# Up-projection of a hybrid layer: high and low words of each weight interleaved in SBUF

## The chip, the cores and the metric

The kernel runs on one core of a Trainium2 chip. The metric is the device time of one execution in microseconds; the time before is 2269.59 us, the median of three runs (2268.82 to 2269.59).

## The reference

One layer of a streaming encoder for 2048 prompt tokens and 8 x 16 sample tokens: mLSTM heads and windowed attention over one input projection, an output projection, a layer norm, and then a convolutional feed-forward part. Only the start of that last part is touched by the change:

```python
def conv_ffn(h, conv_prev, w_up, w_conv, b_conv, w_down):
    T = h.shape[1]
    u = h @ w_up                      # (T, 1024) @ (1024, 2 * 2816)
    ext = jnp.concatenate([conv_prev.astype(u.dtype), u], axis=1)
    c = b_conv + sum(ext[:, j:j + T] * w_conv[j] for j in range(CONV_W))
    a, g = jnp.split(c, 2, axis=-1)
    return (jax.nn.silu(g) * a) @ w_down, ext[:, -(CONV_W - 1):]
```

All inputs and outputs are float32, and so is the product `h @ w_up`.

## The kernel before

The 2048 + 128 tokens are 17 tiles of 128. The kernel has four stages, one after the other: input projection (with mLSTM and attention woven in), output projection, up-projection (`f_ups`), down-projection (`f_downs`). Each float32 product is made of float32r matmuls: `split` (L220) writes a high part of an operand with ScalarE (a cast to float32r, L222) and the remainder with VectorE (a subtraction, L223), and three matmuls add high x high, high x low and low x high in PSUM.

The up-projection goes over three blocks of tokens (`FBLOCKS`: 6, 6 and 5 tiles), and in each block over 22 pairs j of 128 value columns and 128 gate columns of `w_up`. A pair is a 2 x 2 block product (two halves of the contraction, value and gate, two halves of the tokens) done with seven products instead of eight, numbered s = 1 to 7, on sums of the operands. A product (`f_product`, L1894) contracts over 512: four steps k of 128, and at each step three matmuls, with the weights stationary (128 x 128, high, high, low) and half of the block's tokens moving (384 columns, 320 in the last block). That is 12 matmuls a product, 7 x 22 x 3 = 462 products, 5544 matmuls, all at L1902. They go to six PSUM banks, three named `fup` and three named `dps`, used by odd and even pairs in turn.

`self.seq` holds the order of the products, written out by hand (`ORDER`), and the TensorE program follows it. `f_next` (L1806) prepares the weights of one product: it takes the next of ten slots of 1088 words per partition (`f_slot`, of which 1024 words from word 48 on are used) and fills it with the high part and the low part of a [128, 4, 128] quarter, 512 words each. It runs `AHEAD` = 6 products ahead of TensorE in the first block and 8 in the others. Where the weights come from differs:

- In the first block every quarter is split on the chip. Products 6, 5, 7 and 3 use sums of quarters, which VectorE makes first (L1819 to L1822), and what was split for them is also stored to DRAM (`zw`, L1837).
- In the later blocks those four are loaded from `zw` (L1830, 512 KB each), and only products 1, 2 and 4 are split again from the raw weights `wv` and `wg`.

Beside this VectorE makes the sums of the results (`f_evict`), the depthwise convolution (L1960) and the gate (L1986, L1987); ScalarE copies PSUM banks and makes the first term of the convolution (L1958) and the tanh. All loads and stores of the stage are issued by SyncE's queue (SP). `f_written` (L1889) issues two extra matmuls of 512 columns with a weight slot as stationary operand.

Of the kernel before, what the change touches and what calls it, by code (L numbers as in the profile page):

```python
# [8 lines left out]
F32 = mybir.dt.float32  # L9
# [197 lines left out]
class Prog:  # L207
# [1598 lines left out]
    def f_next(self):  # L1806

        nc, V = self.nc, self.nc.vector
        if self.made >= len(self.seq):
            return False  # L1810
        b, j, s = self.seq[self.made]
        self.made += 1
        if s == 1:
            if (b, j) not in self.wr:
                self.f_raw(b, j)
            if b == 0:
                v, g = self.wr[b, j]
                s12, s34 = self.f_slot(48, F32), self.f_slot(48, F32)
                V.tensor_add(s12[:, :4], g[:, :4], g[:, 4:])  # L1819
                V.tensor_sub(s34[:, :4], v[:, :4], g[:, :4])  # L1820
                V.tensor_sub(s12[:, 4:], s12[:, :4], v[:, :4])
                V.tensor_sub(s34[:, 4:], v[:, 4:], s12[:, 4:])  # L1822
                self.wr[b, j] = v, g, s12, s34
        if s == 5 and (b, j) != (len(FBLOCKS) - 1, NFF - 1):
            self.f_raw(b + (j + 1) // NFF, (j + 1) % NFF)
        w = self.f_slot(48).rearrange("p (i k) m -> p i k m", i=2)
        i = SUMS.index(s) if s in SUMS else None
        keep = None if i is None else self.zw[j][i].rearrange("p (i k m) -> p i k m", i=2, k=4)
        if b and i is not None:
            nc.sync.dma_start(w.bitcast(F32), keep)  # L1830
        else:
            r = self.wr[b, j]
            q = {1: lambda: r[0][:, :4], 2: lambda: r[0][:, 4:], 4: lambda: r[1][:, 4:], 5: lambda: r[2][:, :4],
                 6: lambda: r[2][:, 4:], 7: lambda: r[3][:, :4], 3: lambda: r[3][:, 4:]}[s]()
            self.split(w[:, 0], w[:, 1], q)
            if i is not None:
                nc.sync.dma_start(keep, w.bitcast(F32))  # L1837
        self.wc[b, j, s] = w[:, 0], w[:, 1]
        return True

# [395 lines left out]
```

## Time and profile before

| what | value |
|---|---|
| time, median of 3 runs | 2269.59 us |
| the profiled execution: time | 2270.08 us |
| the profiled execution: span from first to last instruction | 2268.3 us |
| granted TensorE clock over the span | 0.999 |
| up-projection matmuls (L1902), first start to last start | 886.8 to 1810.1 us |
| DMA traffic over the span | 631.30 MB, mean 278 GB/s |

The profile gives for each engine the time in which it was busy; PE is the matmuls and PEld the loads of the stationary operand, which run beside them. Both are pipelined: a matmul's own duration is longer than the distance between the starts of two matmuls, so the rate is read from starts or from pieces of the chain that hold many matmuls, not from durations. A group's line gives line, engine, operation, names, shape and count, then busy time, mean duration of one in ns, and the idle time of the engine before them. The chain of work is followed back from the last instruction; its pieces have a start, a length and a count.

### The profile page before, as it was taken

What the parts mean: (1) busy time and instruction counts of PE and PEld (TensorE: products, weight loads), DVE (VectorE), ACT (ScalarE), POOL (GpSimd) and SP (SyncE); (2) the same over time, 40 slices, a digit from 0 to 9 for tenths busy, and PEclk for the clock granted to TensorE, in tenths of its full rate; (3) what the DMA queues carried; (4) which work ended last, traced back from release to release, by engine and by line L of the source; (5) the groups of instructions that cost most, each with busy time, mean ns of one, the idle gap of its engine ahead of it and who ended that gap; (6) DMA issues with size and microseconds to landing.
All of it is one profiled execution on the core that took longest, in us unless ns stands there. A gap on an engine that the chain in (4) does not pass through costs nothing.

```text
span 2268.3 us, 39783 instructions
## 1 busy us (share of the span) xinstructions
PE 2251.2 (99%) x14293; PEld 2081.9 (92%) x14293; DVE 1807.6 (80%) x3069; ACT 1273.1 (56%) x2374; POOL 270.3 (12%) x509
## 2 busy tenths in 40 slices
PE   9999999999999999999999999999999999999998
PEld 8999999999878778999999999999999988888887
DVE  9787687777698888998778777678766787896997
ACT  5453476776776656555656555556555644444452
POOL 0001001000021110211112000003211200100100
PEclk9999999999999999999999999999999999999999
DMA  8888998898997767898777999988998796757752
GB/s 304 315 314 317 317 320 275 277 315 294 331 325 262 275 216 282 305 330 302 279 284 261 308 307 311 314 274 277 316 304 263 253 318 207 255 188 234 247 171 89
DMA packets 302277, 631.30 MB, mean 278 GB/s; under 512 B 47420, under 2 KB 140672, under 8 KB 302080
## 3 DMA queue, kind: packets, MB, share of 16 engines
q1 hardware_dynamic: 296832, 614.01, 78.9%
q0 software_dynamic: 3520, 10.56, 1.5%
q10 hardware_dynamic: 1728, 4.20, 0.5%
q8 instruction: 113, 1.85, 0.3%
q14 instruction: 84, 0.69, 0.1%
HBM read 457.02 MB, written 171.64 MB: 277 GB/s over the span
## 4 chain that ended last, share of the span: by engine, by line
PE 80%; DVE 5%; issue 1%; ACT 1%; DMA 1%; POOL 0%; DVEq 0%; SPq 0%; ACTq 0%; POOLq 0%
PE dps L1902 20%; PE fup L1902 20%; PE dps L726 8%; PE fup L2112 7%; PE dps L2112 7%; PE fht L2112 5%; PE dps L227 2%; PE dps L228 2%; PE dps L229 2%; PE ppo L1372 1%; PE dps L752 1%; PE psc L1327 1%; PE ppt L1366 1%; DVE w L223 1%; PE fht L1724 1%
## 5 line engine op out<-in xcount | busy, mean ns | idle before, releaser
L1902 PE MATMUL fup<-hh,uw 128*128 128x384 f32 (+1 forms) x1848 | 476.8, 327 | 0.0
L1902 PE MATMUL dps<-hh,uw 128*128 128x384 f32 (+1 forms) x1848 | 476.7, 327 | 0.0
L1902 PEld LDWEIGHTS fup<-hh,uw 128*128 128x128 f32 x1848 | 329.6, 188 | 0.1
L1902 PEld LDWEIGHTS dps<-hh,uw 128*128 128x128 f32 x1848 | 329.5, 188 | 0.0
L1902 PE MATMUL fup<-hl,uw 128*128 128x384 f32 (+1 forms) x924 | 301.9, 327 | 1.2 <-DVE hl L223 1.2
L1902 PE MATMUL dps<-hl,uw 128*128 128x384 f32 (+1 forms) x924 | 301.7, 327 | 0.0
L1960 DVE SCALAR_TENSOR_TENSOR cc<-u,cw,cc 128x768 f32<-128x768 f32 (+1 forms) x264 | 258.1, 978 | 38.5 <-ACT cc L1958 32.1
L726 PE MATMUL dps<-w,oh 128*128 128x256 f32 x1344 | 251.2, 283 | 0.2 <-ACT dps L820 0.2
L222 ACT CAST uw<-wraw 128x1024 fp32r<-128x1024 f32 x126 | 123.9, 983 | 216.1 <-PE dps L2112 117.9
L223 DVE TENSOR_TENSOR w<-wraw,w 128x1024 fp32r<-128x1024 f32 (+2 forms) x163 | 186.5, 1150 | 63.8 <-ACT w L222 61.7
L222 ACT CAST w<-wraw 128x1024 fp32r<-128x1024 f32 (+2 forms) x163 | 160.7, 992 | 110.8 <-PE dps L726 55.4
L726 PEld LDWEIGHTS dps<-w,oh 128*128 128x128 f32 x1344 | 209.7, 188 | 11.3 <-issue 8.1
L726 PE MATMUL dps<-w,ol 128*128 128x256 f32 x672 | 187.1, 278 | 0.0
L223 DVE TENSOR_TENSOR uw<-wraw,uw 128x1024 fp32r<-128x1024 f32 x126 | 142.3, 1129 | 53.8 <-ACT uw L222 53.7
L1902 PEld LDWEIGHTS fup<-hl,uw 128*128 128x128 f32 x924 | 173.6, 188 | 1.9 <-DVE hl L223 1.8
L1902 PEld LDWEIGHTS dps<-hl,uw 128*128 128x128 f32 x924 | 173.6, 188 | 0.0
L726 PE MATMUL dps<-oh,w 128*128 128x256 f32 x896 | 167.4, 283 | 2.0 <-ACT mr L1177 0.9
L2112 PE MATMUL fup<-uw,fu 128*128 128x512 f32 x726 | 168.9, 389 | 0.0
L2112 PEld LDWEIGHTS fup<-uw,fu 128*128 128x128 f32 x726 | 136.3, 188 | 28.3
L2112 PE MATMUL dps<-uw,fu 128*128 128x512 f32 x660 | 160.7, 389 | 0.0
L2112 PEld LDWEIGHTS dps<-uw,fu 128*128 128x128 f32 x660 | 123.9, 188 | 25.8
L726 PEld LDWEIGHTS dps<-oh,w 128*128 128x128 f32 x896 | 139.8, 188 | 7.9 <-issue 4.1
(319 smaller groups left out, 4555.8 us busy)
## 6 DMA issues: line engine op xcount, KB each, us to landing
uw<-zw SPq DMA_DIRECT2D x176, 512.0 KB, 5.1
zw<-uw SPq DMA_DIRECT2D x88, 512.0 KB, 3.4
w<-zws SPq DMA_DIRECT2D x72, 512.0 KB, 5.9
wv<-wup SPq DMA_DIRECT2D x66, 512.0 KB, 5.3
wraw<-wi SPq DMA_DIRECT2D x65, 512.0 KB, 5.3
wraw<-zt SPq DMA_DIRECT2D x60, 512.0 KB, 3.8
wraw<-wdn SPq DMA_DIRECT2D x45, 512.0 KB, 3.9
wraw<-wo SPq DMA_DIRECT2D x40, 512.0 KB, 4.4
```

The lines of the kernel that those rows point to most:

```text
L222: nc.scalar.copy(hi, src)
L223: return nc.vector.tensor_sub(lo, src, hi.bitcast(F32)).ins
L227: mm(out, ah, bh, start=start, stop=False)
L228: mm(out, ah, bl, start=False, stop=False)
L229: mm(out, al, bh, start=False, stop=stop)
L726: mm(o, l, r, start=s in (1, 7) and c == k == i == 0, stop=k == 3 and i == 2, skip_group_check=True)
L752: mm(o, x, w, start=k == i == 0, stop=k == KD - 1 and i == 2, skip_group_check=True)
L1327: nc.tensor.matmul(ps[kvh][:, j, :nk], q[rs, j0 + j], k[rs, sel], start=i == 0, stop=i == 2)
L1366: nc.tensor.transpose(pp[:, j * P:(j + 1) * P], scs[j // 2][:, 2 * kvh + j % 2, kt * P:(kt + 1) * P], self.ident)
L1902: mm(ps, l[:, k], r[:, k], start=s in (1, 7) and k == 0 and i == 0, stop=k == 3 and i == 2, skip_group_check=True)
L1960: V.scalar_tensor_tensor(c[:, v], u[:, i:i + n], w[i], c[:, v], op0=ALU.mult, op1=ALU.add)
L2112: mm(ps, l[:, k, c], r[:, k], start=s in (1, 4, 7) and u == 0 and k == 0 and i == 0, stop=u == nu - 1 and k == n - 1 and i == 2, skip_grou ...
```

## The change

Where a slot held 512 words of the high part and behind them 512 words of the low part, it now holds them word by word: high and low part of the same weight are neighbours. The two operands are views of one tile, with a step of two words:

```diff
-        w = self.f_slot(48).rearrange("p (i k) m -> p i k m", i=2)
+        both = self.f_slot(48).rearrange("p k m -> p (k m)")
+        w = both.rearrange("p (k m i) -> p i k m", i=2, k=4)
         i = SUMS.index(s) if s in SUMS else None
-        keep = None if i is None else self.zw[j][i].rearrange("p (i k m) -> p i k m", i=2, k=4)
         if b and i is not None:
-            nc.sync.dma_start(w.bitcast(F32), keep)
+            nc.sync.dma_start(both.bitcast(F32), self.zw[j][i])
         else:
...
             self.split(w[:, 0], w[:, 1], q)
             if i is not None:
-                nc.sync.dma_start(keep, w.bitcast(F32))
+                nc.sync.dma_start(self.zw[j][i], both.bitcast(F32))
         self.wc[b, j, s] = w[:, 0], w[:, 1]
```

So ScalarE's cast (L222) and VectorE's subtraction (L223) write every second word, VectorE also reads the high part that way, TensorE loads its 128 stationary columns from words that are 8 bytes apart, and the two transfers to and from `zw` move the same 4096 bytes per partition in the new order. Instructions, their number and order, buffers and line numbers stay as they are. The other stages keep their layout.

## The prediction

> **What bounds the kernel now.** I read the page's first part, then a table by stretches for the three token blocks of the up-projection, then the chain of work.
>
> ```profile
> span 2268.3 us, 39783 instructions
> PE 2251.2 (99%) x14293; PEld 2081.9 (92%) x14293; DVE 1807.6 (80%) x3069; ACT 1273.1 (56%) x2374; POOL 270.3 (12%) x509
> 886.80:1207.50 320.70, 320.23 (x1864) 319.41 (x1863) 278.01 (x402) 188.78 (x319) 49.66 (x88) 1.00 0.80 296
> 1207.50:1535.00 327.50, 326.80 (x1900) 326.11 (x1899) 246.75 (x288) 178.32 (x278) 39.39 (x89) 1.00 0.89 296
> 1535.00:1810.10 275.10, 275.10 (x1874) 275.09 (x1873) 202.43 (x289) 152.12 (x285) 64.70 (x178) 1.00 0.88 286
> ```
>
> The columns of the last three rows are: stretch, length, busy time of PE, PEld, DVE, ACT and POOL, granted clock, DMA share, GB/s. PE is busy in all of 923.3 us but 1.2. DVE has 42.7, 80.8 and 72.7 us free in the three blocks, ACT 131.9, 149.2 and 123.0. So the stage lasts as long as TensorE's stream, and the question is what sets the distance between two matmuls. The chain of work gives it, in pieces with many matmuls:
>
> ```profile
> 1000.23 4.16 PE fup L1902 x24
> 1803.36 7.04 PE dps L1902 x48
> 1994.90 15.19 PE fup L2112 x67
> ```
>
> 4.16/24 is 173.3 ns with 384 moving columns, 7.04/48 is 146.7 ns with 320, and 15.19/67 is 226.7 ns with 512 columns in the down-projection. The three lie on a line: (226.7 - 146.7)/192 = 0.417 ns a column, and 146.7 - 320 x 0.417 = 13.3 ns that do not grow with the columns. Every matmul has a load of its stationary operand beside it (both counts are 14293). Whether this load is what sets the 146.7 and 173.3 ns is seen from a place with fewer columns, the input projection's 256:
>
> ```profile
> 102.77 0.28 PE L726 MATMUL dps<-w,ol 128*128 128x256 f32 x1
> ...
> 104.82 0.28 PE L726 MATMUL dps<-w,ol 128*128 128x256 f32 x1
> L726 PEld LDWEIGHTS dps<-w,ol 128*128 128x128 f32 x672 | 126.7, 189 | 0.1
> ```
>
> Between these two starts lie 18 matmuls (six groups of three): 113.9 ns each. The load there has the same duration, 189 ns, as the up-projection's 188. So a load of 128 contiguous columns fits into 113.9 ns, and in the up-projection it has 146.7 - 113.9 = 32.8 ns to spare in the last block and 59.4 ns in the first two. The moving operand bounds, not the stationary one.
>
> **The change part by part.** Nothing is added or removed: the same instructions in the same order. Four things get another access pattern.
>
> *The load of the stationary operand, 5544 times.* Its cost by columns shows in three rows with contiguous operands:
>
> ```profile
> L1902 PEld LDWEIGHTS fup<-hh,uw x1848: 187/188/190, 886.5 to 1802.9; 128*128 128x128 f32 x185
> L1372 PEld LDWEIGHTS ppo<-pth,kva x124: 132/134/137, 332.6 to 841.9; 128*64 128x64 f32 x124
> L1464 PEld LDWEIGHTS pnum<-cns,qm x64: 106/110/114, 195.6 to 216.5; 128*32 128x32 f32 x64
> ```
>
> (188 - 110)/96 = 0.81 ns a column, so 104 ns of the 188 are the reading of 128 columns. After the change it reads a word from every 8 bytes: 8 bytes in 0.81 ns, 9.9 bytes of address per ns. No row of this kernel has a stationary operand with a step, so the cost has to be bounded. Lower end: nothing. The nearest row for this is the other operand of the same instruction: the moving stream goes through contiguous words at 4 bytes in 0.417 ns, 9.6 bytes per ns, over hundreds of columns. Memory thus hands TensorE addresses that advance as fast as the stepped load would. Upper end: the load takes twice its 104 ns. Then a matmul could not follow its predecessor within 113.9 + 104 = 218 ns: 3696 matmuls x (218 - 173.3) = 165 us and 1848 x (218 - 146.7) = 132 us, together +297 us. I take nothing, since the nearest row is that of the moving operand, and since a load even 32 ns longer stays hidden beside the moving stream.
>
> The Trainium skill (SBUF — State Buffer, Specifications (TRN2)) says that memory is read in 16-byte lines, that at least two hits per line are needed for full bandwidth, and that each crossing to a new line costs. Stepped fp32 words hit a line exactly twice, so by this rule the load keeps its rate, and the crossings rise from 32 to 64 a load. No run shown so far has such a load.
>
> *The toll of 13.3 ns on each matmul.* If it comes from the load's reading in the way of the moving stream, reading over twice the memory could double it: 5544 x 13.3 = +74 us. If the new order takes the load out of the way, it could go: -74 us. Against a toll of the reading speaks the 256-column place: 113.9 - 256 x 0.417 = 7.2 ns there, with the same 128 columns loaded per matmul. I take no change, and keep +74 and -74 as ends.
>
> *The split.* The rows of the two sides:
>
> ```profile
> L223 DVE TENSOR_TENSOR uw<-uw 128x512 fp32r<-128x512 f32 x86 | 58.8, 686 | 18.7 <-ACT uw L222 18.5
> L223 DVE TENSOR_TENSOR uw<-wv,uw 128x512 fp32r<-128x512 f32 x44 | 30.2, 687 | 8.6 <-ACT uw L222 8.2
> L223 DVE TENSOR_TENSOR uw<-wg,uw 128x512 fp32r<-128x512 f32 x22 | 15.1, 685 | 0.6 <-ACT uw L222 0.6
> L223 DVE TENSOR_TENSOR uw<-wraw,uw 128x1024 fp32r<-128x1024 f32 x105 | 127.9, 1218 | 50.5 <-ACT uw L222 50.4
> L222 ACT CAST uw<-uw 128x512 fp32r<-128x512 f32 x88 | 54.5, 622 | 15.8 <-DVE uw L1820 6.4 <-PE fup L1902 3.2 <-PE dps L1902 2.4
> L222 ACT CAST uw<-wraw 128x1024 fp32r<-128x1024 f32 x105 | 110.8, 1055 | 168.5 <-PE dps L2112 96.8 <-PE fup L2112 61.5 <-issue 5.0
> ```
>
> The first three rows are of the first block alone: 86 + 44 + 22 = 152 splits. Doubling the elements costs DVE 1218 - 686 = 532 ns and ACT 1055 - 622 = 433 ns, about 1.04 and 0.85 ns an element, each no faster than one word at a time. Lower end: nothing. Upper end, again twice the time per element: in the first block 152 x 0.532 = 80.9 us more on DVE against 42.7 us free, which leaves 38.2 us for TensorE to wait; in the other blocks 66 x 0.532 = 35.1 us each, within the 80.8 and 72.7 us free. ACT would get 152 x 0.433 = 65.8 us, within 131.9. I take nothing: at one 4-byte word in 1.04 ns a step of 8 bytes asks for 7.7 bytes of address per ns, less than the moving stream's 9.6. Up to 42.7/152 = 0.28 us more per split is covered by DVE's free time.
>
> *The transfers with* `zw`.
>
> ```profile
> uw<-zw SPq DMA_DIRECT2D x176, 512.0 KB, 5.1
> zw<-uw SPq DMA_DIRECT2D x88, 512.0 KB, 3.4
> ```
>
> 512 KB over 128 partitions are 4096 contiguous bytes each, in SBUF and in DRAM, before and after: nothing, and SP's queue holds the same list.
>
> *Waits.* Today the first matmul of a product needs only the high part, the third the low part. With the words interleaved the two regions overlap as ranges, so the first one may have to wait for DVE as well; behind it on PE is the whole stream. The cover is the lead of the preparation, six products of 12 x 173.3 ns, 12.5 us. It is thinnest at the stage's start:
>
> ```profile
> 885.39 0.68 DVE L223 TENSOR_TENSOR uw<-wv,uw 128x512 fp32r<-128x512 f32 x1
> 886.77 0.34 PE L1902 MATMUL fup<-hh,uw 128*128 128x384 f32 x1
> ```
>
> 886.77 - 886.07 leaves 0.70 us even for the first product. Cost: nothing; without that cover, two matmuls' distance, 0.35 us, per product that is late.
>
> **The sum.** 0 on each line. The profiled execution took 2270.08 us for its span of 2268.3, and its time lies 0.5 us above the median of the runs. I forecast the median unchanged, 2269.6 us. About 0.2% (4.5 us) is what a measurement of this kernel can tell from no change.
>
> **The rivals.**
>
> *The toll grows* (slower). In L1902 the matmul's distance rises by up to another 13.3 ns, because the load now goes through 1024 instead of 512 bytes per partition while the moving operand is being read. It decides as soon as one of the two streams waits for the other at all, since nothing covers a longer distance. For it: the 13.3 ns exist, are the same with 320, 384 and 512 columns, and no row explains them otherwise. Against it: the 7.2 ns at 256 columns. By half of the toll +37 us, 2307 us; by all of it 2343 us. Chance 0.20.
>
> The Trainium skill (TensorE: Matmul & The Clock Gate, Step-by-step: what each phase is for) speaks against this rival: the moving operand and the load have read ports of their own, so that a load takes nothing from a running matmul. By it the 13.3 ns would be something else and would stay.
>
> *The load becomes the bound* (slower). If a stepped load takes more than 32.8 ns longer, the last block pays, beyond 59.4 ns all blocks. A load 80 ns longer gives 3696 x 20.6 + 1848 x 47.2 = 163 us; the doubled one 297 us, 2567 us. For it: the load has only about a quarter to a third of its slot free. Against it: the moving operand's rate of address. Chance 0.16, of which 0.07 below 2400 us.
>
> *DVE becomes the bound in the first block* (slower). With twice the time per element +38 us, 2308 us, from 0.28 us per split on. For it: DVE is busy in 87% of that block, and the stage's start hangs on its splits. Chance 0.08.
>
> *The toll shrinks* (faster). Part or all of 74 us goes, since high and low part of a weight are now read in the same stretch of memory. No row shows a distance under that line at 320 columns or more. 2233 us by half. Chance 0.11.
>
> *The change has no effect on the chip because it does not do what it says*: the views are operands of the very instructions, and no copy stands between; I see no way for that.
>
> **How the numbers follow.** No difference 0.45 (its own range is 2265 to 2274); toll grows 0.20, DVE 0.08, load a little longer 0.07, load much longer 0.09; faster 0.11. From 2265 to 2400 us lie 0.45 + 0.20 + 0.08 + 0.07 = 0.80; outside lie the faster case and the much longer load. Faster by over 0.2%: 0.11. Within: 0.45. Slower: 0.20 + 0.16 + 0.08 = 0.44.
>
> **What would show it.** If I am right, pieces of 24 matmuls at L1902 still last 4.16 us and those of 48 in the last block 7.04, the split's rows stay at 686 and 622 ns, and no wait of PE for L223 grows. If the load is at fault, its row leaves 188 ns, and the last block's 146.7 ns grow first and most. If the toll grows, all three blocks gain the same nanoseconds per matmul. If DVE is at fault, its row grows, PE waits for L223, and only in the first block. I am wrong most simply if a stepped stationary read is not served like the moving one: it is the one cost that no row here bounds closely.

## The result, and the profile after

The changed kernel takes 2275.91 us, the median of seven runs (2274.46 to 2278.63), against 2269.41 us before (seven runs, 2268.41 to 2271.06): 6.5 us more, a ratio of 1.0029 with a 95% interval of 1.0019 to 1.0039. It is slower, by a little more than the 0.2% that I called no difference.

The page of the changed kernel, and its table by the three token blocks, with the same columns as before (the last two stretches are set to where the last block starts and ends now):

```profile
span 2274.2 us, 39783 instructions
PE 2255.2 (99%) x14293; PEld 2086.0 (92%) x14293; DVE 1807.3 (79%) x3069; ACT 1283.7 (56%) x2374; POOL 270.8 (12%) x509
886.80:1207.50 320.70, 320.24 (x1864) 319.54 (x1863) 277.83 (x401) 194.34 (x319) 50.67 (x88) 1.00 0.80 296
1207.50:1535.20 327.70, 326.99 (x1900) 326.41 (x1899) 246.82 (x289) 180.64 (x278) 39.40 (x89) 1.00 0.90 296
1535.20:1816.00 280.80, 280.30 (x1874) 280.04 (x1873) 203.01 (x289) 154.91 (x285) 63.90 (x179) 1.00 0.88 280
```

Counts are the same, and the first two blocks end where they ended. The last one took 275.1 us and takes 280.8 us: 5.7 of the span's 5.9 us arise there. DVE is no busier, ACT has 10.6 us more over the span. The chain of work says what grew:

```profile
1000.23 4.16 PE fup L1902 x24
1809.10 7.17 PE dps L1902 x48
```

With 384 columns 24 matmuls still take 4.16 us, 173.3 ns each. With 320 columns 48 take 7.17 us instead of 7.04: 149.4 ns instead of 146.7. The mean over that block's 1848 matmuls is 2.65 ns more, 4.9 us; it is a mean, for single distances in that block, from start to start, lie mostly between 145 and 155 ns, where they lay between 145 and 148 before. The rest of the block's 5.7 us, 0.8 us, is a single stop near 1602 us, which a second profiled execution (e10 below) does not have. Now the rows of the load and the split:

```profile
L1902 PEld LDWEIGHTS fup<-hh,uw x1848: 192/194/200, 886.5 to 1808.6; 128*128 128x128 f32 x185
L223 DVE TENSOR_TENSOR uw<-uw 128x512 fp32r<-128x512 f32 x88 | 60.2, 686 | 18.6 <-ACT uw L222 18.4
L222 ACT CAST uw<-uw 128x512 fp32r<-128x512 f32 x88 | 58.3, 666 | 15.3 <-DVE uw L1820 6.4 <-PE fup L1902 3.1 <-PE dps L1902 2.1
uw<-zw SPq DMA_DIRECT2D x176, 512.0 KB, 4.9
zw<-uw SPq DMA_DIRECT2D x88, 512.0 KB, 3.3
```

The load's median went from 188 to 194 ns, ScalarE's cast from 622 to 666; VectorE's subtraction stayed at 686, and the transfers land as they did. So there are two candidates: a load that is 6 ns longer beside a stream that I thought had 32.8 ns to spare, and a cast that is 44 ns longer on an engine that is busy in 56% of the span.

### The profile page after: what moved, and what is told of

The parts are those of the page before. It is cut to its first block, busy times and chain, and to the rows that moved or that the text cites. A ratio compares the mean times of both kernels' runs of the same rounds, so it can differ in the third digit from the quotient of the medians.

```text
span 2274.2 us, 39783 instructions
## 1 busy us (share of the span) xinstructions
PE 2255.2 (99%) x14293; PEld 2086.0 (92%) x14293; DVE 1807.3 (79%) x3069; ACT 1283.7 (56%) x2374; POOL 270.8 (12%) x509
## 4 chain that ended last, share of the span: by engine, by line
PE 81%; DVE 5%; issue 1%; ACT 1%; DMA 1%; POOL 0%; DVEq 0%; SPq 0%; ACTq 0%; POOLq 0%
PE dps L1902 20%; PE fup L1902 20%; PE dps L726 8%; PE fup L2112 7%; PE dps L2112 7%; PE fht L2112 5%; PE dps L227 2%; PE dps L229 2%; PE dps L228 2%; PE ppo L1372 1%; PE ppt L1366 1%; PE psc L1327 1%; PE dps L752 1%; DVE w L223 1%; PE fht L1724 1%
## 5 line engine op out<-in xcount | busy, mean ns | idle before, releaser
L1902 PE MATMUL fup<-hh,uw 128*128 128x384 f32 (+1 forms) x1848 | 479.5, 329 | 0.5 <-ACT ub L1931 0.5
L1902 PE MATMUL dps<-hh,uw 128*128 128x384 f32 (+1 forms) x1848 | 479.2, 328 | 0.0
L1902 PEld LDWEIGHTS fup<-hh,uw 128*128 128x128 f32 x1848 | 337.6, 195 | 0.8 <-ACT ub L1931 0.8
L1902 PEld LDWEIGHTS dps<-hh,uw 128*128 128x128 f32 x1848 | 337.5, 195 | 0.0
L1902 PE MATMUL fup<-hl,uw 128*128 128x384 f32 (+1 forms) x924 | 303.3, 328 | 1.2 <-DVE hl L223 1.2
L1902 PE MATMUL dps<-hl,uw 128*128 128x384 f32 (+1 forms) x924 | 303.0, 328 | 0.0
L222 ACT CAST uw<-wraw 128x1024 fp32r<-128x1024 f32 x126 | 123.8, 983 | 216.2 <-PE dps L2112 117.9
L223 DVE TENSOR_TENSOR w<-wraw,w 128x1024 fp32r<-128x1024 f32 (+2 forms) x163 | 186.4, 1149 | 62.9 <-ACT w L222 61.5
L222 ACT CAST w<-wraw 128x1024 fp32r<-128x1024 f32 (+2 forms) x163 | 160.7, 992 | 110.3 <-PE dps L726 51.2
L223 DVE TENSOR_TENSOR uw<-wraw,uw 128x1024 fp32r<-128x1024 f32 x126 | 142.1, 1128 | 53.8 <-ACT uw L222 53.7
L1902 PEld LDWEIGHTS fup<-hl,uw 128*128 128x128 f32 x924 | 180.0, 195 | 1.9 <-DVE hl L223 1.8
L1902 PEld LDWEIGHTS dps<-hl,uw 128*128 128x128 f32 x924 | 180.0, 195 | 0.0
```

Source lines behind the costliest of these rows:

```text
L222: nc.scalar.copy(hi, src)
L223: return nc.vector.tensor_sub(lo, src, hi.bitcast(F32)).ins
L1902: mm(ps, l[:, k], r[:, k], start=s in (1, 7) and k == 0 and i == 0, stop=k == 3 and i == 2, skip_group_check=True)
```

## The experiments

Five theories stand behind the expectations. Theory 1: the stepped load needs about 147 ns from its issue to its matmul and has become the bound of the last block. Theory 2: the longer cast reaches TensorE. Theory 3: a stepped load costs its matmul a few ns of stream, wherever it runs. Theories 4 and 4b came later, and are told at their place. e1, e2, e8 and e9 have 7 to 11 runs each; the others are one execution each, and their argument rests on distances and loads in the profile. Line numbers move by one or three where an edit adds lines.

**e1 and e2: the read alone, the write alone.** e1 writes the parts apart and reads every second word; e2 does the opposite.

```diff
 e1:
-        w = both.rearrange("p (k m i) -> p i k m", i=2, k=4)
+        w = both.rearrange("p (i k m) -> p i k m", i=2, k=4)
...
+        w = both.rearrange("p (k m i) -> p i k m", i=2, k=4)
         self.wc[b, j, s] = w[:, 0], w[:, 1]
 e2:
         w = both.rearrange("p (k m i) -> p i k m", i=2, k=4)
...
+        w = both.rearrange("p (i k m) -> p i k m", i=2, k=4)
         self.wc[b, j, s] = w[:, 0], w[:, 1]
```

> The two parts are written apart as before, but TensorE reads every second word across both, so the products are of mixed words. Theory 1 (the stepped load takes the place of the moving stream as the bound in the last block): all of the loss comes back without the stepped writes, about +5 us (2274), the distance in the last block near 149.4 ns instead of 146.7, ScalarE's cast at 622 ns. Theory 2 (ScalarE's cast, 45 ns longer, comes too late for TensorE): no loss, 2269.4, the distance 146.7 ns. Theory 3 (the stepped reading slows the moving stream itself): +5 us as theory 1.

> The two parts are written word by word as in the changed kernel, but TensorE reads 128 words that lie next to each other, so the products are of mixed words. Theory 1: the time of before, at most +1 us for the wait of 0.8 us on ScalarE that the changed kernel's profile shows at 1602 us; the distance in the last block 146.7 ns, ScalarE's cast near 667 ns. Theory 2: +5 to +6 us. Theory 3: no loss beyond that wait.

e1 took 2275.58 us against 2269.85 of before on the same chip, ratio 1.0024 (1.0014 to 1.0035). e2 took 2269.66, ratio 1.0000 (0.9991 to 1.0009). The last long piece of the chain in e1 and then in e2, and the cast in e2:

```profile
1811.28 7.17 PE dps L1903 x48
```

```profile
1803.00 7.04 PE dps L1903 x48
```

```profile
L222 ACT CAST uw<-uw 128x512 fp32r<-128x512 f32 x88 | 57.9, 662 | 16.7 <-DVE uw L1820 7.3 <-PE fup L1903 3.1 <-DVE uw L223 2.3
```

With the stepped read alone the last block runs at 149.4 ns; with the stepped writes alone it runs at 146.7, although the cast is at 662 ns. The loss is TensorE's read. Theory 2 falls.

**e3 and e4: fewer moving columns.** If the load is the bound, the distance does not shrink with the moving stream. Both leave out 64 of the last block's 320 columns, e3 in the changed kernel, e4 in the kernel before.

```diff
+        c = 256 if b == 2 else h
...
-                mm(ps, l[:, k], r[:, k], start=...
+                mm(ps[:, :c], l[:, k], r[:, k, :c], start=...
```

> The changed kernel, but in the last block only 256 of the 320 moving columns are multiplied (the other columns of that block's result are left out). Theory 1 (the load is the bound there): the distance stays near 149 ns although the moving stream is 27 ns shorter, and the last block gets no shorter: about 2275 us. Theory 3 (the moving stream is slowed by 2 to 3 ns): 113.9 + 2.7, about 117 ns, the block 60 us shorter, 2215 us.

> The kernel before with the same 256 columns in the last block (the rest left out): the control. Both theories: 113 to 114 ns as in the input projection, 1848 x 33 ns = 61 us shorter than before, 2208 us, unless another engine or the transfers become the bound.

Starts of matmuls within the last block, e3 first, then e4:

```profile
1700.09 0.28 PE L1903 MATMUL fup<-hl,uw 128*128 128x256 f32 x1
...
1701.89 0.28 PE L1903 MATMUL fup<-hl,uw 128*128 128x256 f32 x1
```

```profile
1700.54 0.28 PE L1903 MATMUL dps<-hl,uw 128*128 128x256 f32 x1
...
1701.60 0.28 PE L1903 MATMUL dps<-hl,uw 128*128 128x256 f32 x1
```

Between the rows of e3 lie 15 matmuls, 120.0 ns each; between those of e4 nine, 117.8 ns each. Theory 1 falls: a stepped load lets its matmul start every 120 ns, far below the 146.7 ns of 320 columns. The difference of 2.2 ns to the control is of the size that 320 columns show, as theory 3 has it, but e5 and e6 below leave another reading of it. The control surprised as well: 117.8 ns with contiguous loads, where the input projection's place ran at 113.9. The times (2254.16 and 2247.53 us) say little here, for the shorter stream of both has to wait for transfers, as the row of each that holds the longest wait shows (total, times, longest):

```profile
PE fup L1903 <- DMA uw<-zw: 8.2, 4, 3.8
```

```profile
PE fup L1903 <- DMA uw<-zw: 10.1, 5, 4.7
```

**e5 and e6: larger steps.** The parts lie apart as before, and TensorE reads every fourth (e5) or every third word (e6). The cut shows e5; e6 has `both[:, :768]` and `i=3`.

```diff
+        z = both.rearrange("p (k m i) -> p i k m", i=4, k=2)
+        self.wc[b, j, s] = [(lambda k, v=z[:, i]: v[:, k % 2]) for i in range(2)]
...
-                mm(ps, l[:, k], r[:, k], start=...
+                mm(ps, l(k), r[:, k], start=...
```

> The parts are written apart as before, and TensorE reads every fourth word, 16 bytes apart, over two of four quarters of the slot (the products are of mixed words). If the load's cost goes with the 16-byte lines that it touches (32 contiguous, 64 at a step of two, 128 here; 110 and 147 ns from load to matmul give 1.15 ns a line): 110 + 96 x 1.15 + 3 = 223 ns in all blocks, 3696 x 50 + 1848 x 77 = +325 us, 2595 us. If any step costs the same: +5 us, 2274 us, with 149 ns in the last block. If the load is only as long as its row says (a few ns more): +0 to +20 us.

> The same with every third word, 12 bytes apart (the products are of mixed words). If the cost goes with the lines touched (96): 110 + 64 x 1.15 + 3 = 187 ns in all blocks, 3696 x 13.5 + 1848 x 40 = +124 us, 2393 us. If any step costs the same: 2274 us. If what counts is two words per line, as a step of 12 bytes no longer has: between those of a step of two and of four.

The load's row, a piece of the chain with 384 columns and one with 320, of e5 and then of e6:

```profile
L1903 PEld LDWEIGHTS fup<-hh,uw x1848: 308/329/334, 886.1 to 2179.5; 128*128 128x128 f32 x185
```

```profile
1307.10 2.80 PE dps L1903 x12
```

```profile
1905.67 5.60 PE dps L1903 x24
```

```profile
L1903 PEld LDWEIGHTS fup<-hh,uw x1848: 250/252/264, 886.8 to 1870.5; 128*128 128x128 f32 x185
```

```profile
1304.41 4.27 PE dps L1903 x24
```

```profile
1703.53 2.09 PE dps L1903 x12
```

A step of four words makes the load 329 ns, and the matmuls follow each other every 233.3 ns with 384 as with 320 columns: there the load is the bound, and the kernel takes 2650.98 us, 381 more. I had expected 223 ns, from an assumed price per line that rested on theory 1; the size came out near, the ground of it had fallen. A step of three words makes the load 252 ns and the distances 177.9 and 174.2 ns (expected 187), the time 2339.08 us. So 188, 194, 252 and 329 ns are the loads at steps of one to four words: the second word is nearly free, the third and fourth cost 58 and 77 ns. The Trainium skill's rule of two hits per 16-byte line (SBUF — State Buffer, Specifications (TRN2)) puts the border between a step of two and of three words, and the four rows agree.

The distances of the two runs with 320 columns, where the load is the bound, go with the step: 174.2/3 is 58.1 ns for each word of the step, and 233.3/4 is 58.3. An estimate from these two for a step of two words is 2 x 58.2 = 116 ns. That is far below 146.7, as e3 showed, but close to the 120.0 ns of e3: with 256 columns the stepped load may itself be the bound, so the 2.2 ns between e3 and e4 do not prove theory 3.

**e8 and e9: stepped weights in part.** e8 lets products 1, 2 and 4 of the last block lie apart; e9 interleaves only products 1, 2 and 4 of the first two blocks.

```diff
-        w = both.rearrange("p (k m i) -> p i k m", i=2, k=4)
+        w = both.rearrange("p (k m i) -> p i k m" if b < 2 or s in SUMS else "p (i k m) -> p i k m", i=2, k=4)   # e8
+        w = both.rearrange("p (k m i) -> p i k m" if b < 2 and s not in SUMS else "p (i k m) -> p i k m", i=2, k=4)   # e9
```

> The changed kernel, but in the last block the weights of products 1, 2 and 4 lie apart again; products 6, 5, 7 and 3 stay interleaved. Theory 1: in the last block 3 of 7 products go back to 146.7 ns, the others stay near 149.4, so about 4/7 of 5 us, +3 us over before, 2272.3. Theory 2: the casts of the last block go back to 622 ns and those of the first two stay, so all or nothing of the loss by where it arises; the distance in products 6, 5, 7 and 3 would be 146.7.

> Only products 1, 2 and 4 of the first two blocks are interleaved, nothing in the last block. Theory 1: the stepped load stays hidden beside 384 moving columns: the time of before within 1 us, 2269.4 to 2270.4, with loads of 194 ns and a distance of 173.3 ns in those products. Theory 2: part of the loss, since 132 casts are longer: +1 to +3 us. Theory 3: 1584 of the 5544 matmuls would be slowed if the toll held at 384 columns, +4 us.

e9 took 2270.74 us, ratio 1.0004 (0.9995 to 1.0013), e8 2272.02 us, ratio 1.0006 (0.9997 to 1.0015). Neither is clear of no change. The median of e9 is 0.9 us above before, within the 1 us that theory 1 allowed and below the 4 of theory 3 at 384 columns; that of e8 is 2.2 us above, near the 3 of theory 1. The profile of e8 holds something that no theory had. Two stretches of its last block:

```profile
1556.66 3.52 PE dps L1902 x24
1560.18 3.52 PE fup L1902 x24
```

```profile
1700.38 1.79 PE fup L1902 x12
1702.17 1.79 PE dps L1902 x12
1703.96 1.76 PE fup L1902 x12
1705.72 3.55 PE dps L1902 x24
```

Near the block's start one stepped product is slow, at 148.6 ns. From 1544 to 1600 us every product runs at 146.7 ns, also those with stepped loads; then the stream stops once for 0.1 us, and from there on the contiguous products run at 146.7 and the stepped ones at about 149.3. So a stepped load can be free even with 320 columns. e1 has the counterpart with 384 columns:

```profile
948.77 2.12 PE fup L1903 x12
```

```profile
1300.83 4.16 PE fup L1903 x24
```

From 900 to 1076 us its matmuls follow each other every 176.7 ns, and after the first transposes that interrupt them (L1724) every 173.3 ns to the end of that block and through the next. e3 ran at 176.7 ns from 1217 to 1403 us. That gave theory 4: with stepped loads the stream has two paces, and keeps the one in which it last started.

**e10, e11, e12: restarts.** e10 is the changed kernel again. e11 and e12 put one more matmul ahead of product 1 of each pair, in the changed kernel and in the one before.

```diff
+        if s == 1:
+            c = 32 + 8 * j
+            mm(ps[:, :c], wh[:, 0], hh[:, 0, :c], start=True, stop=True, skip_group_check=True)
```

> The changed kernel once more, for a second profiled execution. Theory 4 (with a stepped load the stream of load and matmul has a fast and a slow pace, 173.3 or 176.7 ns with 384 columns and 146.7 or 149.3 with 320, and keeps the one in which it last started until it is stopped): the last block at 149.3 for most of its length; in the first two blocks stretches between two stops at 176.7 may stand or not, so 2274 to 2279 us, with the differences of whole stretches. Theory 3 (a stepped load costs each matmul the same): the same distances as in the first profile everywhere.

> The changed kernel with one more matmul ahead of product 1 of every pair (66 of them, 32 to 200 columns by the pair's number, overwritten by the product's first matmul), so that the stream restarts 66 times at various phases. The matmuls themselves cost some 66 x 0.1 = 7 us. Theory 4: pairs at both paces in all blocks, with 384 columns some at 173.3 and some at 176.7 ns, with 320 some at 146.7 and some at 149.3. Theory 3: 149.3 in every pair of the last block and 173.3 in the others.

> The control: the kernel before with the same 66 matmuls. Theory 4: contiguous loads have the fast pace alone with 320 and 384 columns: 146.7 and 173.3 ns in every pair, apart from the few matmuls behind the added one; about 2277 us.

e10 took 2275.17 us, and its distances are those of the first profile: 173.3 ns in both first blocks, 149.3 in the last. e11 took 2282.99 us and e12 2276.90, 6.1 us apart, about as the kernels are without the added matmuls. A piece of the last block with one of them (L1902) in it, of e11 and then of e12:

```profile
1807.09 0.09 PE dps L1902
1807.18 3.61 PE dps L1905 x24
1810.79 1.79 PE fup L1905 x12
```

```profile
1801.28 0.09 PE dps L1902
1801.37 3.53 PE dps L1905 x24
1804.91 1.76 PE fup L1905 x12
```

Without product 1 itself and without stops, the 22 pairs of the last block have means of 149.1 to 149.5 ns in e11, and the 44 pairs with 384 columns 173.3 to 173.8; e12 has 146.6 to 146.7 and 173.3 to 173.4. Restarts alone do not select the pace, so theory 4 fails as I had put it.

**e13: one contiguous product of seven.**

```diff
-        w = both.rearrange("p (k m i) -> p i k m", i=2, k=4)
+        w = both.rearrange("p (k m i) -> p i k m" if b < 2 or s != 1 else "p (i k m) -> p i k m", i=2, k=4)
```

> The changed kernel, but in the last block the weights of product 1 alone lie apart again, one product of seven. Theory 4b (a stepped load goes on at the pace that the matmuls before it had, and contiguous products bring the fast one): stretches of the last block in which the stepped products run at 146.7 ns too, as the run with products 1, 2 and 4 apart showed from 1544 to 1600 us; 2270 to 2273 us. Theory 3 (each stepped load costs its matmul the same with 320 columns): 146.7 ns in product 1, 149.3 in all others, 6/7 of the loss, 2274 us.

It took 2274.38 us against 2268.83 of before. In the last block product 1 runs at 146.6 ns, and the other six run at 148.7 to 149.6, beside a few products at the block's start. Theory 4b falls, and theory 3 holds for the last block as the rule, with the 56 us of e8 as the exception. "Wherever it runs" does not hold: with 384 columns the stepped loads of the changed kernel go at 173.3 ns, as the contiguous ones do.

## Why the prediction came out as it did

*The forecast.* The median of 2275.91 us lies 1.9 us above the range that I had given to no difference (2265 to 2274) and far below the 2307 us that half of the toll would give. The wide range, 2265 to 2400, holds it because it spans both. No line of the sum gives it, so as far as the mechanism goes, that it fell inside is luck.

*What bounds.* Right: the stage lasts as long as TensorE's stream, and what was lost was lost there.

*The load, "I take nothing".* Half right. It grew by 6 ns, not by 104, and e3 shows that there was room beside the moving stream: a stepped load fits into 120.0 ns, 26.7 less than the last block's 146.7. That the moving operand's rate is the row to go by held for a step of two words, and e5 and e6 show where it ends.

*The toll, "I take no change, and keep +74 and -74 as ends".* This is the step that failed. The 13.3 ns in the last block became 16.0: 2.65 ns x 1848 = 4.9 us of the 6.5. It is nearest to my first rival, but at a fifth of its full size, and only with 320 columns as the rule; I had priced it over all 5544 matmuls and said that all three blocks would gain the same. The reason that I gave for that rival, more memory read beside the moving operand, no run shows. The argument by which I had ruled it out was weak: the 7.2 ns at 256 columns came from one place. The profile of the kernel before has others, at the same line:

```profile
230.04 0.28 PE L726 MATMUL dps<-w,ol 128*128 128x256 f32 x1
...
232.16 0.28 PE L726 MATMUL dps<-w,ol 128*128 128x256 f32 x1
```

Again 18 matmuls lie between the two starts: 117.8 ns each, as in e4, and 117.8 - 106.7 = 11.1 ns that do not grow with the columns. So the remainder is not one fixed number even with contiguous loads. It is not fixed by the program either: here is one stretch of the input projection, which the change does not touch, in the kernel before and then in e10.

```profile
191.96 0.28 PE L726 MATMUL dps<-ol,w 128*128 128x256 f32 x1
...
195.02 0.28 PE L726 MATMUL dps<-ol,w 128*128 128x256 f32 x1
```

```profile
191.78 0.28 PE L726 MATMUL dps<-ol,w 128*128 128x256 f32 x1
...
194.96 0.28 PE L726 MATMUL dps<-ol,w 128*128 128x256 f32 x1
```

Each pair spans 27 matmuls: 113.3 ns each in the kernel before, 117.8 in e10.

The Trainium skill (TensorE: Matmul & The Clock Gate, Step-by-step: what each phase is for) has a load take no read bandwidth from a running matmul. e1 differs from the kernel before only in the step of the load, and so in the values that are multiplied, and the matmuls' distance in the last block rises by 2.7 ns; so the load does reach the stream in some way. Whether the matmul streams more slowly, as that sentence rules out, or starts later after its load, no row tells.

*The split.* DVE as forecast, 686 ns. ACT's cast lengthened by 44 ns, which I had put at nothing; it is covered as the working said, by the free time of ACT, and e2 shows it: 2269.66 us with the longer casts.

*The transfers and the wait for the low part.* As forecast: median landing times as before, and PE waited for the token halves as before. The rows of PE's waits in the changed kernel hold one more, the 0.5 us of the stop near 1602 us:

```profile
PE fup L1902 <- DVE hl L223: 1.2, 2, 0.7
PE fup L1902 <- ACT ub L1931: 0.5, 1, 0.5
```

Ahead of that stop ScalarE's cast waited for a raw weight's transfer, and its copy of `ub` came late behind it. e9, with nothing interleaved in its last block, has the same stop near 1602 us, 1.3 us long. ScalarE's wait in the changed kernel, then in e9, and PE's in e9:

```profile
ACT uw L222 <- DMA wv<-wup: 4.5, 1, 4.5
```

```profile
ACT uw L222 <- DMA wv<-wup: 5.0, 1, 5.0
PE fup L1902 <- ACT ub L1931: 1.1, 1, 1.1
```

Before, the same wait was 3.6 us and in e10 2.2, and neither has the stop. So it goes with a transfer that lands late, not with the longer casts of that block.

*The sum.* 4.9 us are found in both profiles of the changed kernel, and e1 and e2 put them to TensorE's stepped read. The remaining 1.6 of the 6.5 us lie within the spread of its runs. A stretch at 176.7 ns like that of e1 would cost 996 matmuls x 3.3 ns = 3.3 us, and a stop like the one at 1602 us 0.8 us; that these make the upper runs is an inference, since one execution of each program was profiled, and two of the changed kernel.

*What stays open.* What selects the pace, at 146.7 or 149.4 and at 173.3 or 176.7 ns with stepped loads and at 113.3 or 117.8 with contiguous ones and 256 columns, and by what way the load slows the stream.

## What to carry to other kernels

A stationary float32r operand with a step of two words costs next to nothing in the load itself, and one of three or four words a lot: keep the step within 8 bytes. Slack that is read as "the other stream is longer" does not promise a free ride: the distance between two matmuls can still grow by a few ns, and with thousands of them on the bound engine that is the whole effect. Before a distance is used as an argument, read it at several places: 113.9 ns at one place of the input projection was one of two paces. If nothing is gained by interleaving, write and read the parts apart.

## What the runs showed of the hardware that was not expected

The same line runs whole stretches at one of two paces. With stepped loads these are 173.3 or 176.7 ns with 384 columns (e1) and 146.7 or 149.4 with 320 (e8, as means), with contiguous loads 113.3 or 117.8 with 256 (the kernel before). In e1 and e3 the pace changed at a stop of the stream; in e8 it changed once behind a contiguous product, without one. ScalarE's cast of 512 words costs 44 ns more when it writes every second word (666 against 622 ns), while VectorE's subtraction, which reads one operand and writes its result with that step, costs the same (686 ns).
